# Products wider than 128 columns walk their moving operand and their bank in two interleaved halves

## The chip, the core and the metric

The kernel runs on one core of one Trainium2 chip. The metric is the device time of one execution in microseconds, as the median of several runs. The engines of the core work beside each other, each on its own queue: TensorE multiplies matrices (the profile calls the products PE and the loads of their stationary operand PEld), VectorE (DVE) and ScalarE (ACT) work elementwise, GpSimd (POOL) takes some elementwise work, SyncE (SP) issues most DMAs. A matmul holds its stationary operand (up to 128 x 128) in the array, streams the columns of its moving operand past it from SBUF, and adds or writes the result into one bank of PSUM, 512 fp32 columns wide. The profiler records one execution.

## What is computed

One decoder block on x (1024 tokens x 1024 channels, fp32). Two branches read one normalised input, are gated and projected together; then follow a cross-attention into 256 memory tokens, a SwiGLU feed-forward layer and a last norm. Cut to what matters:

```python
u = rms_norm(h, norm_mix)
proj = u @ w_in                                    # u_ssm, q, k, v, f_logit, gate_logits
y_ssm = gelu(s5_ssm(u_ssm, ...))                   # diagonal state-space scan in 32 groups
glu_a, glu_b = split(y_ssm @ w_glu)
out_a = glu_a * sigmoid(glu_b)
out_b = forgetting_attention(q, k, v, f_logit + b_forget) @ w_fox_o   # causal, 8 heads of 64
h = h + (gate_a * out_a + gate_b * out_b) @ w_mix_out
h = h + memory_cross_attention(rms_norm(h), rms_norm(mem), w_mem_q, w_mem_kv, w_mem_o)
f_a, f_b = split(rms_norm(h) @ w_ffn_in)           # 1024 -> 2 x 2816
h = h + (silu(f_a) * f_b) @ w_ffn_out
out = rms_norm(h, norm_final)
```

## The kernel before

Every fp32 operand of a large product is split into a high part, rounded to the type fp32r that TensorE takes in one pass, and a low part, the rest (`Block.split`, L186: a ScalarE cast and a VectorE subtraction). A product is then three fp32r matmuls into one bank: high x high, high x low, low x high (`Block.mm3`, L175, with its three matmuls on L177, L178 and L179). `gemm_t` (L181) calls `mm3` for each 128-row slice of the contraction.

The work runs in stages, one behind the other with some overlap: the norms and transposes with the first projections (`stage_in`, whose order is written out by hand in `ORDER_IN`; there the profile puts all operations on L126, the line of the helper that keeps the order), gates and state-space branch (`stage_ssm`), the forgetting attention (`Fox`), the gated merge, mixing projection and cross-attention (`stage_tail`), and the feed-forward layer at its end. The mixing projection and both feed-forward projections use seven block products instead of eight, so they have matmul lines of their own: `mix_mm` (L660), `prod` (L1014, 22 hidden blocks x 7 block products x 12 matmuls) and `o_mm` (L1161, 7 block products x 11 x 12 matmuls). In the attention, `row_max` (L1767) computes scores once for the row maximum, `scores` (L1794 and L1795) computes them again transposed, and `values_hi` and `values_lo` (L1819, L1820, L1826) multiply the exponentials by the values. There the stationary operand has 64 or 65 columns, and on the diagonal a product has 128, 256, 384 or 512 moving columns. `values_of_v` has products of 264 and 256 columns, `keys` and `mem_scores` of 256. All others of these lines have 512.

In all of them the moving operand is a contiguous row of fp32 elements in each SBUF partition, and so is the stretch of the bank that it is written to. Bank use rotates over the names `mm`, `sc`, `pv` and `misc` (L130). Transposes and the small fp32 products of the state-space branch (L1504, L1510, L1535, L1578, L1579), with 128 columns or fewer, call the engine directly, and so does `warm` (L253), a few bf16 products of 256 columns at the start that use no result.

Which matmul waits for which operand is put in by the framework, from the tiles that it reads and writes.

Of the kernel before, what the change touches and what calls it, by code (L numbers as in the profile page):

```python
# [19 lines left out]
P = 128  # L20
# [46 lines left out]
def f32(ap):  # L67
    return ap.bitcast(F32)
# [60 lines left out]
class Block:  # L129
    BANKS = {"mm": 3, "sc": 2, "pv": 2, "misc": 1}  # L130

    def __init__(self, ctx, tc):
        self.tc, self.nc = tc, tc.nc
        nc = self.nc
        self.V, self.A, self.G, self.T, self.S = nc.vector, nc.scalar, nc.gpsimd, nc.tensor, nc.sync
        self.const = ctx.enter_context(tc.tile_pool(name="const", bufs=1))
# [32 lines left out]
    def wblock(self, w, k0, nk, c0, nc_, pool_lo=False, behind=None):  # L169
# [2 lines left out]
        hi, lo = self.wload([(0, (nk, nc_), src)], nk * nc_, pool_lo, behind)  # L172
        return tuple(t[:, :nk * nc_].rearrange("p (k c) -> p k c", k=nk) for t in (hi, lo))

    def mm3(self, ps, lh, ll, rh, rl, first, last):  # L175
        T = self.T
        T.matmul(ps, lh, rh, start=first, stop=False)  # L177
        T.matmul(ps, lh, rl, start=False, stop=False)  # L178
        T.matmul(ps, ll, rh, start=False, stop=last)  # L179

    def gemm_t(self, ps, wh, wl, act, h, nk, k0=0):  # L181
        for k in range(nk):
# [49 lines left out]
    def turn(self, xs, b, bank):  # L232

        ps = self.bank(bank)
        for k in range(4):
            self.T.transpose(ps[:, k * P:(k + 1) * P], xs[:, (4 * b + k) * P:(4 * b + k + 1) * P], self.ident)
        return ps
# [15 lines left out]
    def warm(self, n):  # L253
# [3 lines left out]
        for _ in range(n):  # L257
            self.T.matmul(ps[:, :2 * P], one[:, :P], one, start=True, stop=True)

# [313 lines left out]
def stage_tail(B, big, s2, sh, x, glu, aT, gate_d, kv_d, sums_d, w_fox_o, w_mix_out, g_mq, w_mem_q, w_mem_o, g_ffn,  # L573
               w_ffn_in, w_ffn_out, g_fin, out):
    nc, V, A, G, T, S, small, ident = B.nc, B.V, B.A, B.G, B.T, B.S, B.small, B.ident
# [5 lines left out]
    def slot(dt=F32, name="t"):  # L581
        return s2.tile([P, D], dt, tag="t", bufs=NS2, name=name)
# [69 lines left out]
    def mix_mm(n, i):  # L652
        ps = msets[n in (2, 7, 4)][i]
        for kk in range(2):
            wh, wl = mixw[n][kk]
            hi, lo = [a[kk][:, :, i * P:(i + 1) * P]
                      for a in part[(None, "A11", "A12", "S4", "A22", "S1", "S2", "S3")[n]]]
            for k in range(2):
                for m, (l_, r_) in enumerate(((hi, wh), (hi, wl), (lo, wh))):
                    T.matmul(ps, l_[:, k, :], r_[:, k, :], start=n in (1, 2, 7) and kk == k == m == 0,  # L660
                             stop=kk == k == 1 and m == 2, skip_group_check=True)

    def mix_add(n, i):
# [77 lines left out]
    for i in range(2):  # L741
        mix_mm(1, i)
    minuend(7)
    fox_part(6)
    mix_mm(1, 2)
    mix_weights(2)
    fox_part(7)
    mix_mm(1, 3)
    msets.append([B.bank(t_) for t_ in ("sc", "sc", "pv", "pv")])

# [56 lines left out]
    kth, ktl, vh, vl = [slot(F32R, "kv") for _ in range(4)]  # L807
# [200 lines left out]
    def prod(j, n, ps, first):  # L1008
        wh, wl = [t_.rearrange("p (k c) -> p k c", k=4) for t_ in wts.pop((j, n))]
        hi, lo = comb[(None, "A11", "A12", "S4", "A22", "S1", "S2", "S3")[n]]  # L1010
        for k in range(4):
            rh, rl = hi[k // 2][:, k % 2, :], lo[k // 2][:, k % 2, :]
            for i, (l_, r_) in enumerate(((wh, rh), (wh, rl), (wl, rh))):
                T.matmul(ps, l_[:, k, :], r_, start=first and k == 0 and i == 0, stop=k == 3 and i == 2,  # L1014
                         skip_group_check=True)

    def start(j):
        b1, b2 = ev[j, "b1"], _ = B.bank("mm"), B.bank("sc")
        prod(j, 1, b1, True)
        a0 = ev[j, "a0"] = sh.half("a0")  # L1020
        A.copy(a0, b1)
        prod(j, 2, b2, True)
        V.tensor_add(a0, a0, b2)
        A.activation(a0, a0, AF.Silu)

    def middle(j):
        b1 = ev[j, "b1"]
        b3 = ev[j, "b3"] = B.bank("pv")
        prod(j, 6, b1, False)
        a1 = ev[j, "a1"] = sh.half("a1")  # L1030
        A.copy(a1, b1)
        prod(j, 7, b3, True)
        prod(j, 5, b1, False)
        c1 = ev[j, "c1"] = sh.half("c1")
        ev["last"] = A.copy(c1, b1)
        V.scalar_tensor_tensor(out=c1, in0=c1, scalar=-1.0, in1=b3, op0=ALU.mult, op1=ALU.subtract)
# [118 lines left out]
    def o_mm(m, i):  # L1155
        n, p = seq[m]
        hi, lo = ops[m]
        ps = sets[n in (2, 7, 4)][i]
        gi = slice(i * P, (i + 1) * P)
        for k, (l_, r_) in enumerate(((hi, hi), (hi, lo), (lo, hi))):  # L1160
            T.matmul(ps, l_[:, gi], r_[:, 512:], start=n < 3 and p == 0 and k == 0 or n == 7 and p == 0 and k == 0,  # L1161
                     stop=p == NP - 1 and k == 2, skip_group_check=True)

    def o_add(n, i):
# [55 lines left out]
    for i in range(4):  # L1220
# [4 lines left out]
        r = refine() if i else None  # L1225
# [9 lines left out]
class Glu:  # L1235
# [11 lines left out]
    def product(self, j, h, b):  # L1247
        ps = self.B.bank("mm" if b == 0 else None)
        self.B.gemm_t(ps, *self.w[j], self.yT, h, 4, k0=4 * b)
        if j not in self.out:  # L1250
            self.out[j] = self.sh.tmp("sg")

        return ps.rearrange("p (t c) -> p t c", t=4), \
            self.out[j].rearrange("p (c t) -> p t c", t=8)[:, 4 * h:4 * h + 4, :]
# [338 lines left out]
class Fox:  # L1593
# [158 lines left out]
    def row_max(self, h):  # L1752

        B = self.B
        K1, K2, Q1, Q2 = self.hb[h % 2]

        def unit(qb, b):  # L1760
            if qb == 0:
                self.mc[h] = B.small.tile([P, 2, NT], F32, name="mc")
                B.V.memset(self.mc[h][:, 1, :], -3.0e38)
            mc = self.mc[h]
            n = min(512, (qb + 1) * P - 512 * b)
            ps = B.bank("mm")
            B.T.matmul(ps[:, :n], Q1[0:68, qb * P:(qb + 1) * P], K1[0:68, 512 * b:512 * b + n], start=True, stop=True)  # L1767
            if b == qb // 4:
                B.V.tensor_tensor_reduce(out=B.junk[:, :n], in0=ps[:, :n], in1=self.tri[:, 512 - n:512], scale=1.0,
                                         scalar=-3.0e38, op0=ALU.add, op1=ALU.max, accum_out=mc[:, 0, qb:qb + 1])  # L1770
            else:
                B.V.tensor_reduce(out=mc[:, 1, qb:qb + 1], in_=ps, axis=AX.X, op=ALU.max)

        return [lambda qb=qb, b=b: unit(qb, b) for qb in range(NT) for b in range(qb // 4 + 1)]
# [11 lines left out]
    def scores(self, h, qc, kt):  # L1786
        B, fp = self.B, self.fp
        V, A, G, T = B.V, B.A, B.G, B.T
        K1, K2, Q1, Q2 = self.hb[h % 2]
        off = max(0, kt * P - 512 * qc)  # L1790
        q = slice(512 * qc + off, 512 * qc + 512)
        k = slice(kt * P, (kt + 1) * P)
        ps = B.bank("sc")
        T.matmul(ps[:, off:], K1[0:69, k], Q1[0:69, q], start=True, stop=False)  # L1794
        T.matmul(ps[:, off:], K2[:, k], Q2[:, q], start=False, stop=True)  # L1795
        if kt * P >= 512 * qc:
            V.tensor_add(ps[:, off:off + P], ps[:, off:off + P], self.trk)  # L1797
        ph = self.sh.half("ph", F32R)
        pl = fp.tile([P, 512], F32R, tag="pl", bufs=4, name="pl")
        pf = self.sh.half("pf")  # L1800
        self.exp = A.activation(pf[:, off:], ps[:, off:], AF.Exp)  # L1801
        if (qc, kt) in ((0, 2), (1, 0), (1, 2), (1, 4)):
            self.mark = V.tensor_copy(ph[:, off:], pf[:, off:])  # L1803
            G.tensor_sub(pl[:, off:], pf[:, off:], f32(ph[:, off:]))  # L1804
        else:
            A.copy(ph[:, off:], pf[:, off:])  # L1806
            V.tensor_sub(pl[:, off:], pf[:, off:], f32(ph[:, off:]))  # L1807
        self.hi_todo.append((h, qc, kt, off, ph, pl))

    def values_hi(self):  # L1810
        u = h, qc, kt, off, ph, pl = self.hi_todo.pop(0)
        self.lo_todo.append(u)
        if kt == 0:
            if qc == 0:
                self.num[h] = self.fp.tile([65, L], F32, tag="num", name="num")
            self.pvs[h, qc] = self.B.bank("pv")
        ps = self.pvs[h, qc]
        va, vl = self.vh[kt // 2][:, kt % 2, h, :], self.vl[kt // 2][:, kt % 2, h * DH:(h + 1) * DH]
        self.B.T.matmul(ps[0:65, off:], va, ph[:, off:], start=kt == 0, stop=False)  # L1819
        self.B.T.matmul(ps[0:64, off:], vl, ph[:, off:], start=False, stop=False)  # L1820

    def values_lo(self):
        h, qc, kt, off, ph, pl = self.lo_todo.pop(0)
        ps = self.pvs[h, qc]
        last = kt == 4 * qc + 3
        self.B.T.matmul(ps[0:65, off:], self.vh[kt // 2][:, kt % 2, h, :], pl[:, off:], start=False, stop=last)  # L1826
        if last:
            self.B.A.copy(self.num[h][:, 512 * qc:512 * qc + 512], ps[0:65, :])
            if qc == 1:
                self.finish(h)  # L1830
# [158 lines left out]
```

## Time and profile before

| | us |
|---|---|
| median of three runs | 1555.63 (1554.66 to 1558.96) |
| span of the profiled execution, first to last instruction | 1552.1 |
| TensorE products busy in it | 1516.8 |
| TensorE loads of stationary operands busy | 1247.0 |
| VectorE busy | 1056.2 |
| ScalarE busy | 672.7 |
| GpSimd busy | 244.2 |

The profiled execution's span is 3.5 us under the median of the runs; what lies around the first and the last instruction is in the runs' time and not in the span. Busy time of TensorE is the time in which at least one matmul is under way. Matmuls overlap: one begins while the one before it is still draining, and their ends are modelled, so the mean duration that a group of matmuls shows is longer than the step from one start to the next. The step from start to start is what counts for time; it is read from the order of time (starts in the timeline, or the length of a run of matmuls in the chain of work that ended last divided by their number). The trace names the shape of each matmul as stationary rows * columns, then the moving operand's partitions x columns.

### The profile page before, as it was taken

What the parts mean: (1) busy time and instruction counts of PE and PEld (TensorE: products, weight loads), DVE (VectorE), ACT (ScalarE), POOL (GpSimd) and SP (SyncE); (2) the same over time, 40 slices, a digit from 0 to 9 for tenths busy, and PEclk for the clock granted to TensorE, in tenths of its full rate; (3) what the DMA queues carried; (4) which work ended last, traced back from release to release, by engine and by line L of the source; (5) the groups of instructions that cost most, each with busy time, mean ns of one, the idle gap of its engine ahead of it and who ended that gap; (6) DMA issues with size and microseconds to landing.
All of it is one profiled execution on the core that took longest, in us unless ns stands there. A gap on an engine that the chain in (4) does not pass through costs nothing.

```text
span 1552.1 us, 20558 instructions
## 1 busy us (share of the span) xinstructions
PE 1516.8 (98%) x7271; PEld 1247.0 (80%) x7271; DVE 1056.2 (68%) x1895; ACT 672.7 (43%) x1202; POOL 244.2 (16%) x323
## 2 busy tenths in 40 slices
PE   8999999999999899999999999999999999999997
PEld 7787888898777668888888778888888888888886
DVE  7666855554788686788756787777777776566555
ACT  6424333423666653444445654333333333354343
POOL 1045432200212123210102100000000000101001
PEclk9999999999999999999999999999999999999999
DMA  9465657642113647778421375454555554896642
GB/s 296 119 136 110 190 158 152 189 131 29 35 36 65 163 111 244 248 236 320 136 95 55 136 265 207 160 161 158 163 160 160 161 163 145 297 385 218 192 161 109
DMA packets 203177, 258.19 MB, mean 166 GB/s; under 512 B 36457, under 2 KB 127497, under 8 KB 202562
## 3 DMA queue, kind: packets, MB, share of 16 engines
q1 hardware_dynamic: 195874, 240.10, 51.7%
q10 hardware_dynamic: 7200, 16.78, 2.8%
q8 instruction: 57, 0.93, 0.2%
q14 instruction: 46, 0.38, 0.1%
HBM read 175.56 MB, written 83.20 MB: 167 GB/s over the span
## 4 chain that ended last, share of the span: by engine, by line
PE 78%; DVE 8%; DMA 5%; issue 3%; POOL 3%; ACT 2%; SPq 1%; POOLq 0%; ACTq 0%; DVEq 0%
PE mm L1014 15%; PE pv L1014 8%; PE mm L177 6%; PE mm L178 5%; PE mm L179 5%; PE mm L1161 5%; PE sc L1161 4%; PE mm L126 4%; PE sc L1014 3%; PE pv L1161 3%; PE sc L178 2%; PE sc L177 2%; PE sc L179 2%; PE misc L1161 2%; PE pv L178 1%
## 5 line engine op out<-in xcount | busy, mean ns | idle before, releaser
L188 DVE TENSOR_TENSOR wlo<-raw,whi 128x1024 fp32r<-128x1024 f32 (+2 forms) x119 | 127.1, 1070 | 90.9 <-ACT whi L187 90.6
L187 ACT CAST whi<-raw 128x1024 fp32r<-128x1024 f32 (+2 forms) x119 | 107.1, 904 | 116.8 <-DMA raw<-in_w_ffn_in_dram 25.4
L188 DVE TENSOR_TENSOR ol<-or,oh 128x1024 fp32r<-128x1024 f32 x73 | 91.9, 1266 | 67.1 <-ACT oh L187 66.0
L187 ACT CAST oh<-or 128x1024 fp32r<-128x1024 f32 x73 | 76.7, 1053 | 99.2 <-PE mm L1161 33.3
L177 PE MATMUL mm<-uh,whi 128*128 128x512 f32 x280 | 111.7, 399 | 0.5 <-ACT whi L187 0.5
L179 PE MATMUL mm<-uh,wlo 128*128 128x512 f32 x280 | 109.9, 393 | 0.5 <-DVE wlo L188 0.5
L178 PE MATMUL mm<-ul,whi 128*128 128x512 f32 x280 | 110.3, 394 | 0.0
L1046 POOL TENSOR_TENSOR g<-a,c 128x512 f32<-128x512 f32 x22 | 36.2, 1644 | 381.7 <-ACT a L1045 362.6
L1804 POOL TENSOR_TENSOR pl<-pf,ph 128x512 fp32r<-128x512 f32 (+1 forms) x32 | 39.7, 1240 | 241.6 <-DVE ph L1803 195.4
L206 POOL TENSOR_TENSOR r<-ms,mhalf 128x1 f32<-128x1 f32 (+1 forms) x30 | 20.5, 686 | 330.3 <-DVE ms L202 261.0
L1801 ACT ACTIVATE pf<-sc 128x512 f32<-128x512 f32 (+1 forms) x96 | 46.5, 490 | 45.8 <-DVE sc L1797 26.7
L179 PEld LDWEIGHTS mm<-uh,wlo 128*128 128x128 f32 x280 | 52.9, 189 | 12.3 <-DVE wlo L188 1.5
L177 PEld LDWEIGHTS mm<-uh,whi 128*128 128x128 f32 x280 | 53.0, 189 | 10.5 <-ACT whi L187 0.9
L178 PEld LDWEIGHTS mm<-ul,whi 128*128 128x128 f32 x280 | 53.1, 189 | 8.7
L1014 PE MATMUL pv<-S3h,we 128*128 128x512 f32 x176 | 58.2, 390 | 0.1
L1274 POOL TENSOR_TENSOR sg<-sg,ga 128x512 f32<-128x512 f32 x16 | 31.2, 1971 | 69.8 <-DMA ga<-gate_d 40.9
L1807 DVE TENSOR_TENSOR pl<-pf,ph 128x512 fp32r<-128x512 f32 (+2 forms) x64 | 35.0, 548 | 10.1 <-ACT ph L1806 9.3
L1161 PE MATMUL mm<-oh 128*128 128x512 f32 x106 | 41.2, 389 | 0.0
L1161 PE MATMUL mm<-oh,ol 128*128 128x512 f32 x106 | 41.2, 389 | 0.0
L1161 PE MATMUL mm<-ol,oh 128*128 128x512 f32 x106 | 41.2, 389 | 0.0
L177 PE MATMUL mm<-yh,whi 128*128 128x512 f32 x104 | 40.8, 393 | 0.0
L177 PE MATMUL sc<-uh,whi 128*128 128x512 f32 x104 | 40.8, 392 | 0.0
(714 smaller groups left out, 4673.4 us busy)
## 6 DMA issues: line engine op xcount, KB each, us to landing
or<-c_d SPq DMA_DIRECT2D x77, 256.0 KB
wo<-in_w_ffn_out_dram SPq DMA_DIRECT2D x22, 512.0 KB
c_d<-g SPq DMA_DIRECT2D x44, 256.0 KB
t_d<-wo SPq DMA_DIRECT2D x44, 256.0 KB
or<-t_d SPq DMA_DIRECT2D x44, 256.0 KB
raw<-in_w_ffn_in_dram SPq DMA_DIRECT2D x20, 512.0 KB
rawb<-in_w_ffn_in_dram SPq DMA_DIRECT2D x20, 512.0 KB
raw<-in_w_in_dram SPq DMA_DIRECT2D x18, 512.0 KB
```

The costliest lines, as they stand in the source:

```text
L126: return lambda *a, **k: self.tc.keep_in_program_order(op(*a, **k))
L177: T.matmul(ps, lh, rh, start=first, stop=False)
L178: T.matmul(ps, lh, rl, start=False, stop=False)
L179: T.matmul(ps, ll, rh, start=False, stop=last)
L187: self.copied = self.A.copy(hi, src)
L188: self.lowered = (self.G if pool_lo else self.V).tensor_sub(lo, src, f32(hi))
L1014: T.matmul(ps, l_[:, k, :], r_, start=first and k == 0 and i == 0, stop=k == 3 and i == 2, skip_group_check=True)
L1046: G.tensor_mul(g[:, 512:], a1, c1)
L1161: T.matmul(ps, l_[:, gi], r_[:, 512:], start=n < 3 and p == 0 and k == 0 or n == 7 and p == 0 and k == 0, stop=p == NP - 1 and k == 2, ski ...
L1801: self.exp = A.activation(pf[:, off:], ps[:, off:], AF.Exp)
L1804: G.tensor_sub(pl[:, off:], pf[:, off:], f32(ph[:, off:]))
L1807: V.tensor_sub(pl[:, off:], pf[:, off:], f32(ph[:, off:]))
```

## The change

A new method `product` takes the place of the direct call of the engine's `matmul`. Where the result has over 128 columns, it hands the engine the same bank and the same moving operand with another order of columns: the n columns are seen as two halves of n/4 pairs each, and the walk goes pair by pair, one pair of the first half, then one of the second half. For n = 512 the order of columns is 0, 1, 256, 257, 2, 3, 258, 259 and so on. Both sides have the same order, so that each result lands where it did. Number and order of the instructions, the stationary operands, the tiles and everything on the other engines stay.

```diff
+    def product(self, ps, l, r, start, stop, **kw):
+
+        n = ps.shape[-1]
+        if n > P and len(r.shape) == 2:
+            ps, r = (ap.rearrange("p (b a c) -> p a b c", b=2, c=2) for ap in (ps, r))
+        self.T.matmul(ps, l, r, start=start, stop=stop, **kw)
+
     def mm3(self, ps, lh, ll, rh, rl, first, last):
-        T = self.T
-        T.matmul(ps, lh, rh, start=first, stop=False)
-        T.matmul(ps, lh, rl, start=False, stop=False)
-        T.matmul(ps, ll, rh, start=False, stop=last)
+        self.product(ps, lh, rh, first, False)
+        self.product(ps, lh, rl, False, False)
+        self.product(ps, ll, rh, False, last)
...
-                    T.matmul(ps, l_[:, k, :], r_[:, k, :], start=n in (1, 2, 7) and kk == k == m == 0,
+                    B.product(ps, l_[:, k, :], r_[:, k, :], start=n in (1, 2, 7) and kk == k == m == 0,
...
-                T.matmul(ps, l_[:, k, :], r_, start=first and k == 0 and i == 0, stop=k == 3 and i == 2,
+                B.product(ps, l_[:, k, :], r_, start=first and k == 0 and i == 0, stop=k == 3 and i == 2,
...
-            T.matmul(ps, l_[:, gi], r_[:, 512:], start=n < 3 and p == 0 and k == 0 or n == 7 and p == 0 and k == 0,
+            B.product(ps, l_[:, gi], r_[:, 512:], start=n < 3 and p == 0 and k == 0 or n == 7 and p == 0 and k == 0,
...
-        T.matmul(ps[:, off:], K1[0:69, k], Q1[0:69, q], start=True, stop=False)
-        T.matmul(ps[:, off:], K2[:, k], Q2[:, q], start=False, stop=True)
+        self.B.product(ps[:, off:], K1[0:69, k], Q1[0:69, q], start=True, stop=False)
+        self.B.product(ps[:, off:], K2[:, k], Q2[:, q], start=False, stop=True)
```

The calls on L1767, L1819, L1820 and L1826 are replaced in the same way.

More of the change, by code (lines that the diff above doesn't have):

```diff
@@ L1766, in unit @@
             ps = B.bank("mm")
-            B.T.matmul(ps[:, :n], Q1[0:68, qb * P:(qb + 1) * P], K1[0:68, 512 * b:512 * b + n], start=True, stop=True)
+            B.product(ps[:, :n], Q1[0:68, qb * P:(qb + 1) * P], K1[0:68, 512 * b:512 * b + n], start=True, stop=True)
             if b == qb // 4:
@@ L1818, in values_hi @@
         va, vl = self.vh[kt // 2][:, kt % 2, h, :], self.vl[kt // 2][:, kt % 2, h * DH:(h + 1) * DH]
-        self.B.T.matmul(ps[0:65, off:], va, ph[:, off:], start=kt == 0, stop=False)
-        self.B.T.matmul(ps[0:64, off:], vl, ph[:, off:], start=False, stop=False)
+        self.B.product(ps[0:65, off:], va, ph[:, off:], start=kt == 0, stop=False)
+        self.B.product(ps[0:64, off:], vl, ph[:, off:], start=False, stop=False)
     def values_lo(self):
@@ L1825, in values_lo @@
         last = kt == 4 * qc + 3
-        self.B.T.matmul(ps[0:65, off:], self.vh[kt // 2][:, kt % 2, h, :], pl[:, off:], start=False, stop=last)
+        self.B.product(ps[0:65, off:], self.vh[kt // 2][:, kt % 2, h, :], pl[:, off:], start=False, stop=last)
         if last:
```

## The prediction

> **What bounds the kernel.** I read the page first (busy shares, chain), then busy time by stretches, then the chain in order of time.
>
> ```profile
> span 1552.1 us, 20558 instructions
> ...
> PE 1516.8 (98%) x7271; PEld 1247.0 (80%) x7271; DVE 1056.2 (68%) x1895; ACT 672.7 (43%) x1202; POOL 244.2 (16%) x323
> ...
> PE 78%; DVE 8%; DMA 5%; issue 3%; POOL 3%; ACT 2%; SPq 1%; POOLq 0%; ACTq 0%; DVEq 0%
> ```
>
> TensorE products are under way in 1516.8 of 1552.1 us and hold 78% of the chain. All other engines together can give back 35 us at most. By stretches (columns: us, then busy us and number for PE, PEld, DVE, ACT, POOL, then granted clock, DMA share, GB/s):
>
> ```profile
> 0.00:380.00 380.00, 365.83 (x1990) 311.71 (x1991) 230.19 (x498) 142.98 (x244) 96.14 (x209) 1.00 0.61 154
> 380.00:600.00 220.00, 212.00 (x1020) 160.15 (x1020) 164.53 (x387) 130.56 (x248) 40.40 (x33) 0.99 0.36 90
> 600.00:912.00 312.00, 308.56 (x1481) 254.67 (x1479) 234.28 (x416) 148.50 (x332) 57.50 (x47) 1.00 0.55 184
> 912.00:1330.00 418.00, 416.51 (x1842) 343.70 (x1842) 298.49 (x440) 158.78 (x269) 34.43 (x22) 1.00 0.53 175
> 1330.00:1552.00 222.00, 213.89 (x944) 176.74 (x942) 128.74 (x157) 91.83 (x112) 15.72 (x13) 0.99 0.64 223
> ```
>
> In no stretch is another engine busy above 76%, and the clock is granted in full. So the step from one product to the next sets the time. It is read from the chain in order of time (start, length, what):
>
> ```profile
> 1002.51 5.44 PE mm L1014 x24
> ...
> 1535.73 4.09 PE sc L1161 x18
> ```
>
> 24 products of 512 columns take 5.44 us, 18 take 4.09: **0.2267 us a product** in both. Traffic does not move it: the same number of products goes through 100 us with the DMA share at 0.85 as at 0.48.
>
> ```profile
> 1100.00:1200.00 100.00, 100.00 (x442) 82.78 (x442) 71.64 (x101) 35.34 (x56) 7.93 (x5) 1.00 0.48 154
> ...
> 1300.00:1400.00 100.00, 100.00 (x442) 82.66 (x441) 61.88 (x67) 41.72 (x52) 11.96 (x7) 1.00 0.85 303
> ```
>
> **What a column could cost.** The timeline has a few bf16 products of 256 columns that read half the bytes per column, one alone and a group of six:
>
> ```profile
> 11.23 0.27 PE L126 MATMUL mm<-ident 128*128 128x256 bf16 x1
> ...
> 11.23 0.82 PE L126 MATMUL mm<-ident 128*128 128x256 bf16 x6
> ```
>
> Five steps take 0.82 - 0.27 = 0.55 us, 0.110 each. Two of those are 0.220 us for 512 columns, 7 ns under the fp32r product. The attention has fp32r products with narrow stationary operands:
>
> ```profile
> 482.21 0.28 PE L1819 MATMUL pv<-ph,vhi 128*65 128x256 f32 x1
> 482.32 0.28 PE L1820 MATMUL pv<-ph,vlo 128*64 128x256 f32 x1
> 482.44 0.34 PE L1826 MATMUL pv<-pl,vhi 128*65 128x384 f32 x1
> ...
> 483.31 0.22 PE L1819 MATMUL pv<-ph,vhi 128*65 128x128 f32 x1
> 483.37 0.23 PE L1820 MATMUL pv<-ph,vlo 128*64 128x128 f32 x1
> 483.44 0.28 PE L1826 MATMUL pv<-pl,vhi 128*65 128x256 f32 x1
> 483.55 0.39 PE L177 MATMUL mm<-uh,whi 128*128 128x512 f32 x1
> ```
>
> From start to start: 128 columns 0.065 us (two steps in 0.13), 256 columns 0.115 (0.23 for two), 512 columns 0.2267. From 256 to 512 that is 0.1117 us, 0.436 ns a column, with 2 x 0.115 - 0.2267 = 3 ns left over for the handover. Taking the same 3 ns once from the two bf16 steps gives 0.220 - 0.003 = 0.217 us for 512 columns. So a 512-column product has a **surplus of some 10 ns** that grows with its columns, whatever the width of its stationary operand. It thus sits in the walk along the row, which is what the change alters. Two-digit times leave it uncertain by about 3 ns.
>
> The Trainium skill ("TensorE: Matmul & The Clock Gate", section "Back-to-back issue gap") has a warm product at columns / 2.4 + 2.5 ns, 215.8 ns for 512. The row says 226.7 for fp32r, so the trace disagrees for this type; by the page's figure the surplus would be 10.9 ns.
>
> **The change part by part.** It removes and adds no instruction, wait or transfer; it moves the order of columns within products of over 128. The stationary loads stay, and none of the moved products has another queue.
>
> How many: `prod`, `o_mm` and one of the lines of `mm3`, each over the whole span (count in brackets):
>
> ```profile
> 0.00:1552.00 1552.00, 421.06 (x1848) 346.32 (x1848) 1.00 0.55 166
> ...
> 0.00:1552.00 1552.00, 209.77 (x924) 173.43 (x924) 1.00 0.55 166
> ...
> 0.00:1552.00 1552.00, 330.30 (x880) 165.71 (x880) 1.00 0.55 166
> ```
>
> Products of 512 columns: 1848 + 924, `mix_mm` 7 x 4 x 12 = 336, L177 to L179 3 x 880 less 192 of 264 and 288 of 256 columns = 2160, `stage_in` 240, attention 6 lines x 48 = 288. Sum 5796. Besides, 96 of 384 and 672 of 256 or 264.
>
> No row shows a moving operand or a bank walked in pieces, so the price of the new order is bounded. Downward: the whole surplus goes, 10.7 ns (226.7 - 216; I put the floor of 0.217 at 0.216 since both bf16 steps are rounded). Upward: the nearest rows are ScalarE copies of 512 elements, all contiguous, written to SBUF eight elements apart, and read from PSUM eight apart:
>
> ```profile
> L1021 ACT COPY a<-mm 128x512 f32<-128x512 f32 x22 | 12.9, 585 | 20.6 <-PE mm L1014 20.6
> ...
> L1261 ACT COPY sg<-mm 128x512 f32<-128x512 f32 x8 | 9.0, 1156 | 0.0
> ...
> L126 ACT COPY us<-mm 128x512 f32<-128x512 f32 x8 | 4.7, 596 | 10.7 <-PE mm L126 10.7
> ```
>
> Single elements cost 1156 / 585 = 1.98 times on the SBUF side and 1.02 times on the PSUM side. Pairs make half as many jumps: an estimate of 1.49 times at worst, 338 ns a product. The ends are thus -10.7 and +111 ns. I take **-10.7**, because the surplus is proportional to the walk, independent of traffic and absent with half the bytes per column: it looks like consecutive columns that meet in one unit of memory, and two alternating regions 1 KB apart relieve that. This is a choice, not a measurement.
>
> Sum: 5796 x 10.7 ns = 62.0 us. The 96 of 384 columns give 5 ns each, 0.5 us. The 672 narrow ones with 128 stationary columns step in 0.120, 5 ns above the 0.115 of the narrow stationary operand, so something else than the walk is late there; 3 ns each, 2.0 us:
>
> ```profile
> 345.39 0.12 PE mm L177
> 345.51 0.12 PE mm L178
> ```
>
> Off the path: in 380 to 600 us the attention's exponentials and row maxima release TensorE (8 us without a product), and I count half of its gain of some 8 us, -4. Up to 100 us first loads and norms are awaited: -3. In the feed-forward layer nothing comes late: VectorE would go from 298.49/418 = 71% to 298.49/399 = 75%, DMA from 0.53 to 0.56. The stationary loads still fit:
>
> ```profile
> L1014 PEld LDWEIGHTS pv<-S3h,we 128*128 128x128 f32 x176 | 33.0, 188 | 7.4 <-ACT S3h L187 0.5
> ```
>
> 188 ns lies below 216 as it did below 227; where this cover fails, the gain stops at the load. Total 62.0 + 0.5 + 2.0 - 4 - 3 = 57.5: span 1552.1 - 57.5 = 1494.6, and with the 3.5 us by which the runs' median exceeds the span, **1498 us**.
>
> **Rivals.** *A, nothing measurable.* The surplus is a rate, so many bytes per ns from SBUF, or a per-column price of fp32r itself, and order does not enter; or the pattern is turned back into a plain one before it reaches the chip. For it: the step is constant to three digits over hundreds of us, as a rate would be. Against: nothing that the trace shows. 1555.6 us.
>
> *B, slower: each jump between the halves is paid.* The place is the fetch of the moving operand: two neighbouring pairs were one stretch of memory, now they lie 1 KB apart, and 512 columns make 255 jumps. It decides from a price of 10.7 / 255 = 0.04 ns a jump. If the surplus is paid for entering a stretch, and each stretch is now entered twice as often, it doubles: 5796 x 10.7 = +62 us, 1618 (B1). If pairs cost what half of ScalarE's excess says, 5796 x 111 ns = +643 us, 2199 (B2). For it: L1261. Against: L126 reads a bank in steps at 1.02.
>
> The Trainium skill speaks for B in "PSUM — Partial Sum Buffer" (Specifications): 8-byte lines, and any non-contiguous pattern slows matmuls significantly. "Advanced Engine Details and Errata" (PSUM Cachelines) asks only that every two consecutive elements be contiguous, and its section SBUF Cachelines for two hits on a 16-byte line; pairs meet both, which would be A. No row of this trace decides between the sentences.
>
> **How the numbers follow.** Forecast 0.45; A 0.26; B 0.29, of which B1 and prices near it 0.14 and B2 and beyond 0.15. About 0.3% (5 us) is what a measurement can tell from no change here. Faster 0.45, same 0.26, slower 0.29. The forecast's own range is 1484 (all 5796 at 11.2 ns, the others at 8, nothing lost: 65 + 6 = 71 us) to 1545 (one sixth of the gain). Cases of both signs are open, so the range for 8 in 10 reaches through A and B1: 1484 to 1640; B2 stays out.
>
> **What would show it.** Chain: 24 products of L1014 in 5.2 us (forecast), 5.44 (A), 5.7 (B1), 8.1 (B2). The 128-column steps of 0.065 must not move. TensorE's busy time should fall by about what the span falls, and in 380 to 600 us by less per product. Wrong would be: a step of 512 columns that does not change, a surplus that stays while 256-column products gain, or loads of stationary operands that end after the product before them.

## The result, and the profile after

The changed kernel takes 2172.14 us (median of 4 runs, 2169.94 to 2172.32) where the kernel before takes 1557.26 (4 runs beside them, 1554.66 to 1558.96): a ratio of 1.395, with a 95% interval of 1.392 to 1.397. The forecast was 1498 us with a range of 1484 to 1640; the time lies outside of it, on the slow side. Medians in this document are of all runs; ratios leave out one run, of `e6_sixtyfours`, which took 6047.91 us.

The page of the changed kernel, in the same lines as the page before (busy time and number of instructions by engine, then the chain that ended last):

```profile
span 2168.1 us, 20567 instructions
...
PE 2153.8 (99%) x7271; PEld 1327.8 (61%) x7271; DVE 1067.2 (49%) x1895; ACT 675.9 (31%) x1202; POOL 232.4 (11%) x323
...
PE 98%; DVE 1%; issue 1%; ACT 0%; POOL 0%; DMA 0%; POOLq 0%; DVEq 0%; ACTq 0%
```

The same 7271 products and loads, and the other engines do the same work in the same time (VectorE 1067.2 us against 1056.2, ScalarE 675.9 against 672.7). All of the new time is in TensorE's products, which now hold 98% of the chain instead of 78%. The chain in order of time shows the step (start, length, what; `product` has put all of these calls on L180):

```profile
1415.94 4.00 PE pv L180 x12
1419.94 8.00 PE mm L180 x24
```

24 products of 512 columns take 8.00 us where they took 5.44: **0.3333 us a product** against 0.2267, 106.7 ns more, or 0.417 ns for each of the 256 pairs. Nothing else is late, as the next stretches show: 301 products go through 100 us whether VectorE is busy for 51 of them or for 36 (columns as in the stretches shown of before).

```profile
1300.00:1400.00 100.00, 100.00 (x301) 58.50 (x300) 51.40 (x72) 25.75 (x41) 6.36 (x4) 1.00 0.37 118
...
2000.00:2100.00 100.00, 100.00 (x301) 58.50 (x300) 35.53 (x33) 28.95 (x34) 0.00 (x0) 1.00 0.40 131
```

Products that the change leaves alone hardly moved. The timeline of the attention has 128 columns at 0.065 us (two steps from 561.68 to 561.81), as before, while 256 columns went from 0.115 to about 0.165 (558.12 to 558.45). Over all products of 128 columns with 64 or 65 stationary ones, the median step behind another of 128 columns is 60 ns in both traces, and behind a wider product it went from 59 to 67 ns:

```profile
558.12 0.34 PE L180 MATMUL pv<-ph,vhi 128*65 128x256 f32 x1
558.29 0.34 PE L180 MATMUL pv<-ph,vlo 128*64 128x256 f32 x1
558.45 0.42 PE L180 MATMUL pv<-pl,vhi 128*65 128x384 f32 x1
...
561.68 0.23 PE L180 MATMUL pv<-ph,vhi 128*65 128x128 f32 x1
561.75 0.23 PE L180 MATMUL pv<-ph,vlo 128*64 128x128 f32 x1
561.81 0.34 PE L180 MATMUL pv<-pl,vhi 128*65 128x256 f32 x1
```

The steps from start to start, added up by width in both traces, account for the whole difference of the spans: products of 512 columns 1353.2 to 1941.1 us (+587.8), of 256 columns 63.3 to 82.5 (+19.2), of 264 columns 23.2 to 32.6 (+9.4), of 384 columns 21.1 to 24.9 (+3.9), the rest -4.3; together +616.0, and 2168.1 - 1552.1 = 616.0.

### The profile page after: what moved, and what is told of

Read it like the earlier page. It is cut to its first block, busy times and chain, and to the rows that moved or that the text cites. A ratio compares the mean times of both kernels' runs of the same rounds, so it can differ in the third digit from the quotient of the medians.

```text
span 2168.1 us, 20567 instructions
## 1 busy us (share of the span) xinstructions
PE 2153.8 (99%) x7271; PEld 1327.8 (61%) x7271; DVE 1067.2 (49%) x1895; ACT 675.9 (31%) x1202; POOL 232.4 (11%) x323
## 4 chain that ended last, share of the span: by engine, by line
PE 98%; DVE 1%; issue 1%; ACT 0%; POOL 0%; DMA 0%; POOLq 0%; DVEq 0%; ACTq 0%
PE mm L180 48%; PE sc L180 21%; PE pv L180 19%; PE mm L126 4%; PE misc L180 3%; PE sc L126 1%; PE misc L845 0%; PE pv L1585 0%; PE pv L1541 0%; PE pv L1584 0%; PE misc L1516 0%; PE misc L242 0%; PE pv L126 0%; PE misc L126 0%; PE pv L242 0%
## 5 line engine op out<-in xcount | busy, mean ns | idle before, releaser
L180 PE MATMUL mm<-uh,whi 128*128 128x512 f32 x280 | 143.0, 511 | 0.0
L180 PE MATMUL mm<-ul,whi 128*128 128x512 f32 x280 | 142.1, 507 | 0.0
L180 PE MATMUL mm<-uh,wlo 128*128 128x512 f32 x280 | 141.7, 507 | 0.0
L1052 POOL TENSOR_TENSOR g<-a,c 128x512 f32<-128x512 f32 x22 | 35.3, 1604 | 574.4 <-ACT a L1051 574.4
L180 PE MATMUL pv<-S3h,we 128*128 128x512 f32 x176 | 77.6, 502 | 0.0
L180 PEld LDWEIGHTS mm<-uh,wlo 128*128 128x128 f32 x280 | 55.0, 196 | 36.9 <-issue 1.1
L180 PEld LDWEIGHTS mm<-uh,whi 128*128 128x128 f32 x280 | 54.9, 196 | 32.6 <-DVE mc L1775 0.4
L180 PEld LDWEIGHTS mm<-ul,whi 128*128 128x128 f32 x280 | 54.9, 196 | 31.3 <-issue 0.5
L180 PE MATMUL mm<-oh 128*128 128x512 f32 x106 | 53.2, 502 | 0.0
L180 PE MATMUL mm<-ol,oh 128*128 128x512 f32 x106 | 53.2, 502 | 0.0
L180 PE MATMUL mm<-oh,ol 128*128 128x512 f32 x106 | 53.2, 502 | 0.0
L180 PE MATMUL sc<-uh,whi 128*128 128x512 f32 x104 | 53.2, 512 | 0.0
L180 PE MATMUL sc<-ul,whi 128*128 128x512 f32 x104 | 53.1, 510 | 0.0
L180 PE MATMUL sc<-uh,wlo 128*128 128x512 f32 x104 | 53.1, 510 | 0.0
L180 PE MATMUL mm<-yh,whi 128*128 128x512 f32 x104 | 52.3, 503 | 0.0
```

The source lines that it names most:

```text
L180: self.T.matmul(ps, l, r, start=start, stop=stop, **kw)
L1052: G.tensor_mul(g[:, 512:], a1, c1)
```

## The experiments

The theory after the result was that each change of place within the walk costs TensorE time. Three questions were open: on which side it is paid (the read of the moving operand from SBUF or the write to the bank), what is counted (jumps, or pieces of memory fetched), and whether another order could win the 10 ns that the plain walk has above 0.216 us.

The two feed-forward projections have seven block products each, with 132 products of the out projection in a row and 12 of the in projection at a time. So one kernel can give each block product an order of its own, and its step is read from the trace. In the rows below, a stretch of the out projection counts the products under way in it, one or two more than its length divided by the step; the mean step behind it is that of 120 products from start to start. Steps within the in projection are the length of 12 products in the chain, divided by 12. In these runs all other products walk plainly; `e3_fours` and `e6_sixtyfours` instead change one number of the changed kernel. Each was run once, but for `e6_sixtyfours` with ten runs.

### Which side pays (e1_sides)

```diff
-        n = ps.shape[-1]
-        if n > P and len(r.shape) == 2:
-            ps, r = (ap.rearrange("p (b a c) -> p a b c", b=2, c=2) for ap in (ps, r))
+        r, ps = [self.walk(ap, o) for ap, o in zip((r, ps), order)]
...
+ORDER_FFN_IN = {1: ('', ''), 2: ('h4', ''), 6: ('', 'h4'), 7: ('h8', ''), 5: ('', 'h8'), 3: ('h32', 'h32'), 4: ('h64', 'h64')}
+ORDER_FFN_OUT = {1: ('', ''), 2: ('h2', ''), 6: ('', 'h2'), 7: ('h2', 'h2'), 5: ('h4', 'h4'), 4: ('h8', 'h8'), 3: ('h16', 'h16')}
```

For each block product stands the order of the read, then that of the write: empty is the plain walk, `h4` takes groups of four columns from the two halves in turn, as the change does with two.

> All products walk plainly, as before the change, except those of the two feed-forward lines, where each of the seven block products has an order of its own; one-sided orders put the result's columns in other places, which changes values and not times. Feed-forward out: block product 1 plain, 2 pairs on the read side (SBUF) only, 6 pairs on the write side (PSUM) only, 7 pairs on both, 5 fours on both, 4 eights on both, 3 sixteens on both. Feed-forward in: 1 plain, 2 fours read only, 6 fours written only, 7 eights read only, 5 eights written only, 3 thirty-twos on both, 4 sixty-fours on both. The changed kernel's 512-column step of 0.3333 us against 0.2267 is 256 jumps at 0.417 ns, one TensorE cycle each. Theory R (the read pays per jump): pairs read only 0.333, written only 0.227, fours read only 0.280, written only 0.227, eights read only 0.253. Theory W (the bank pays per jump): the same with read and written exchanged. Theory M (a jump costs on the slower of both sides, either alone is enough): 0.333 for all three kinds of pairs. Theory P (it is the pattern of three dimensions, not the jumps): every order but the plain one 0.333. By jumps on both sides: fours 0.280, eights 0.253, sixteens 0.240, thirty-twos 0.233, sixty-fours 0.230.

The out projection by stretches, in the order of its block products 1, 2, 6, 7, 5, 4, 3:

```profile
1350.00:1375.00 25.00, 25.00 (x112) 20.68 (x111) 13.03 (x14) 5.90 (x6) 2.14 (x1) 1.00 0.85 312
1385.00:1415.00 30.00, 30.00 (x90) 17.45 (x89) 12.72 (x11) 10.09 (x10) 0.00 (x0) 1.00 0.87 315
1425.00:1450.00 25.00, 25.00 (x112) 20.71 (x111) 15.91 (x12) 10.95 (x12) 4.21 (x2) 1.00 0.71 227
1460.00:1490.00 30.00, 30.00 (x90) 17.47 (x89) 8.59 (x7) 7.40 (x7) 0.00 (x0) 1.00 0.41 125
1500.00:1530.00 30.00, 30.00 (x122) 22.68 (x121) 12.60 (x12) 11.17 (x11) 0.00 (x0) 1.00 0.54 170
1535.00:1560.00 25.00, 25.00 (x104) 19.51 (x103) 11.03 (x9) 8.83 (x9) 0.00 (x0) 1.00 0.46 147
1565.00:1590.00 25.00, 25.00 (x106) 19.80 (x105) 11.99 (x27) 5.22 (x11) 2.06 (x3) 1.00 0.23 85
```

Compare the first with the third row: 112 products in 25 us whether the bank is written plainly or by pairs, a mean step of 226.7 ns in both. Compare the second with the fourth: 90 in 30 us, 340.0 ns, whether the bank joins in or not. **The read pays all of it and the write nothing**: theory R has the side right, W and M fall. The in projection says the same of larger groups (block products 5 and 1 together, then 2, 3, 4, 6, 7):

```profile
1006.19 5.45 PE mm L180 x24
1011.64 3.01 PE sc L180 x12
1014.65 2.84 PE mm L180 x12
1017.49 2.72 PE pv L180 x12
1020.21 2.72 PE mm L180 x12
1022.93 2.92 PE pv L180 x12
```

Fours written take 2.72 us for 12, eights written and the plain ones 5.45 for 24, as ever; fours read take 3.01, eights read 2.92, thirty-twos 2.84 and sixty-fours 2.72. The pattern of three dimensions as such (theory P) falls with the sixty-fours. But the price is not proportional to the jumps either, as theory R had it (0.280 for fours, 0.253 for eights): pairs cost 106.7 to 113 ns for 256 jumps, fours 23 ns for 128 (250.0), eights 17 for 64 (243.3), sixteens 13 for 32 (240.0). Something sets pairs apart from all the rest.

### Steps in place of halves, and rereading (e2_steps)

```diff
+        if kind == "s":
+            return ap.rearrange("p (a b c) -> p b a c", b=n // 2, c=2)
+        if kind == "k":
+            return ap[:, :n].unsqueeze(1).to_broadcast([P, 512 // n, n])
...
+ORDER_FFN_IN = {1: ('', ''), 2: ('s4', 's4'), 6: ('s8', 's8'), 7: ('s16', 's16'), 5: ('s4', ''), 3: ('', 's4'), 4: ('s16', '')}
+ORDER_FFN_OUT = {1: ('', ''), 2: ('k2', ''), 6: ('k4', ''), 7: ('k16', ''), 5: ('k64', ''), 4: ('', 's16'), 3: ('s64', 's64')}
```

`s4` walks pairs at a step of four columns, in two passes; `k2` reads the first two columns again and again.

> As the run before, with other orders on the feed-forward lines; those that reread a few columns leave the rest of the operand out of the product. Feed-forward in: block product 1 plain, 2 pairs at a step of four columns in two passes on both sides, 6 at a step of eight in four passes, 7 at a step of sixteen in eight passes, 5 step four read only, 3 step four written only, 4 step sixteen read only. Feed-forward out: 1 plain, 2 reads the same two columns 256 times, 6 the same four 128 times, 7 the same sixteen 32 times, 5 the same sixty-four 8 times (the bank is written plainly), 4 step sixteen written only, 3 pairs of halves 64 wide at a step of sixty-four on both. If a jump costs the same whatever its distance, every order of pairs has 0.333 on the side that pays. If only far jumps pay, those at a step of four columns stay at 0.227. If the read pays for each new 16 bytes beyond what a plain walk fetches, steps of four already pay in full. Rereading: if what is left over the clock in the plain walk (0.2267 against 0.2133) is paid for entering new memory on the read side, the same two or four columns give 0.216; if it is paid on the write side or per product, 0.227; if going back is a jump like any other, two columns give 0.333, four 0.280, sixteen 0.240, sixty-four 0.230.

The in projection (block products 2, 3, 4, 6, 7, then 5 and 1 together):

```profile
1075.44 5.43 PE sc L180 x12
1080.87 2.74 PE mm L180 x12
1083.61 5.18 PE pv L180 x12
1088.79 5.54 PE mm L180 x12
1094.33 5.18 PE pv L180 x12
1099.51 8.15 PE mm L180 x24
```

Pairs at a step of four columns take 5.43 us for 12, 452 ns each: worse than the far jumps between halves, and **twice the plain walk**. Written at that step, the bank again costs nothing (2.74). A step of eight has 461 ns, of sixteen 431, and it does not matter whether the bank joins (block products 4 and 7 have 5.18 both). So near jumps are not cheaper; what is lost looks like the other half of what a fetch brings. The third of the three expectations, that steps of four already pay in full, had the direction, and none had the size. The dearest order of all is `s64`, pairs at a step of sixty-four columns on both sides, with a mean step of 486.7 ns, more than twice the plain walk; no run has its write side alone.

```profile
1810.00:1870.00 60.00, 60.00 (x124) 25.58 (x123) 15.44 (x37) 7.33 (x13) 3.33 (x6) 1.00 0.12 44
```

Of the rereading block products, those that read the same two or four columns step in 216.5 ns, 117 in 25 us; here are the plain one, the two and the four columns:

```profile
1630.00:1655.00 25.00, 25.00 (x112) 20.68 (x111) 12.61 (x14) 6.33 (x7) 2.14 (x1) 1.00 0.90 320
1660.00:1685.00 25.00, 25.00 (x117) 21.88 (x116) 16.34 (x14) 12.44 (x12) 0.00 (x0) 1.00 1.05 391
1690.00:1715.00 25.00, 25.00 (x117) 21.85 (x117) 16.55 (x13) 11.50 (x13) 4.45 (x3) 1.00 0.75 248
```

When only two or four columns are reread, the 10 ns of surplus are gone. So they do belong to the read of the moving operand. That they are the price of walking through memory at all, and not of walking in a row, is the reading of all runs together: no order tried that reads 512 different columns came below the plain step.

### Fours throughout (e3_fours)

```diff
-            ps, r = (ap.rearrange("p (b a c) -> p a b c", b=2, c=2) for ap in (ps, r))
+            ps, r = (ap.rearrange("p (b a c) -> p a b c", b=2, c=4) for ap in (ps, r))
```

> The changed kernel with groups of four columns in place of pairs on both sides, in all products of over 128 columns: 128 jumps in 512 columns. If jumps are what costs, half of the excess: 5796 x 53 ns = 309 us over before, span about 1860. If it is lines of 16 bytes fetched twice that cost, fours fetch each once: span about 1552. If it is the three-dimensional pattern: as the changed kernel, 2168.

One run took 1676.07 us, beside 1561.34 of the kernel before. The step is 250.0 ns in both projections: 12 products in 3.00 us.

```profile
1117.11 3.00 PE sc L180 x12
1120.11 3.00 PE mm L180 x12
```

Neither of the simple predictions met it: half of the jumps would have left some 1860 us, fetches of 16 bytes alone 1552. Doubling the group took away four fifths of the excess, which suits the filling of 16 bytes as the larger part, and something smaller for the change of stream stays.

### What is fetched (e4_reads)

```diff
+        if kind == "q":
+            return ap.rearrange("p (b a c) -> p a b c", b=4, c=n)
+        if kind == "t":
+            return ap.rearrange("p (a b c) -> p b a c", b=2, c=n)
...
+            at = 512 - SHIFT.get(n, 0)
+            l_ = l_[:, :1].to_broadcast([P, P]) if n in CONST else l_[:, gi]
+            B.product(ps, l_, r_[:, at:at + 512], order=ORDER_FFN_OUT[n], ...)
```

`q2` takes pairs in turn from four quarters, `t4` every second group of four columns and then the others; `SHIFT` begins the row so many columns earlier, and `CONST` names the block products whose stationary is one column repeated.

> As the two runs before, all on the read side only; values change with it. Feed-forward in: block product 1 rereads the same eight columns, 2 the same thirty-two; 6, 7, 5, 3 and 4 read every second group of 4, 8, 16, 32 and 64 columns in a first pass and the others in a second. Feed-forward out: 1 plain with one stationary column repeated 128 times, 2 pairs of halves with the same, 6 pairs in turn from four quarters, 7 fours from four quarters, 5, 4 and 3 plain but from 2, 4 and 16 columns earlier in the tile. Theory F (the read fetches a unit of 16 bytes in 1.667 ns and keeps only the last): groups of 4 and more at a step fetch no unit twice and stay at 0.227; pairs from quarters cost 256 units, 0.44; fours from quarters 0.227. Theory J (each jump costs 0.417 ns as in the halves): groups of 4 at a step 0.28, of 8 0.253, of 16 0.240; pairs from quarters 0.333, fours 0.28. Theory U (the unit is larger, and a group that does not fill it wastes the rest): groups at a step cost up to twice 0.2133, some 0.44, until the group fills the unit, 0.227 from there on. The surplus of the plain walk: if it comes from the stationary load's reads, 0.216 with one repeated stationary column; if it hangs on where the row begins, it changes with the shift; else 0.227 in all four. Rereading eight columns 0.216, thirty-two 0.227 or above.

Two stretches of the out projection, pairs from quarters and fours from quarters:

```profile
1425.00:1475.00 50.00, 50.00 (x114) 23.39 (x113) 15.45 (x12) 10.17 (x12) 3.43 (x2) 1.00 0.37 122
1485.00:1515.00 30.00, 30.00 (x114) 21.85 (x113) 11.97 (x11) 9.96 (x10) 0.00 (x0) 1.00 0.52 172
```

114 products take 50 us in one and 30 us in the other: 443.3 ns against 268.0. Theory F had 440 and 227, theory J 333 and 280. So F has the pairs, and the fours, which J has nearly, cost 41 ns more than F allows. The walks in two passes decide against J (block products 4, 6 and 7 of the in projection, which read every second group of 64, 4 and 8 columns):

```profile
1020.14 2.76 PE pv L181 x12
1022.90 2.77 PE mm L181 x12
1025.67 2.80 PE pv L181 x12
```

Every second group of 4, 8, 16, 32 and 64 columns steps in 231, 233, 240, 237 and 230 ns, near the plain 227, where J had 280 for the fours. So the unit is not larger than four columns, and theory U falls as well. Pairs from the two halves with one repeated stationary column, block product 2, took 326.7 ns. The surplus of the plain walk hangs neither on the stationary load (231 with one repeated stationary column) nor on the row's beginning (230 to 233 from 2, 4 and 16 columns earlier). Eight columns reread had 215 and thirty-two 237.7.

### Distance, and groups of 64 (e5_apart, e6_sixtyfours)

`e5_apart` takes its two streams of 256 columns from places further apart in the tile; `e6_sixtyfours` is the changed kernel with `c=64` in products whose width is a multiple of 128.

> Read side only, values changed by it: two streams of 256 columns, taken in turn, that lie further apart than the halves' 256 columns. Feed-forward out, pairs: distance 256 (control), 260, 264, 272, 288, 384 and 512 columns for block products 1, 2, 6, 7, 5, 4, 3. Feed-forward in, distance 512: groups of 2, 4, 8, 16, 32, 64 columns for block products 1, 2, 6, 7, 5, 3; 4 plain. Theory F, the read fetches 16 bytes in four TensorE cycles (1.667 ns): pairs from halves had 0.333 to 0.340, which is 192 fetches for 128 units, so half of the second visits still find their unit. If what is kept depends on the place of the two units against each other, the step changes with the distance between 0.227 (all kept, 128 fetches) and 0.440 (none kept, 256). If it is a matter of the order of visits alone, all distances have 0.333 to 0.340. Of groups at distance 512: 0.25, 0.243, 0.24, 0.237, 0.227 for 4, 8, 16, 32, 64 as from halves if the distance does not enter. If alternation relieves a conflict at some distance, as the prediction had it, one of them lies below 0.2267.

By stretches of 35 us, pairs at the distances of 256, 264 and 512 columns:

```profile
1385.00:1420.00 35.00, 35.00 (x105) 20.34 (x104) 11.93 (x13) 10.61 (x10) 0.00 (x0) 1.00 1.01 363
...
1470.00:1505.00 35.00, 35.00 (x108) 20.87 (x108) 15.30 (x12) 10.34 (x12) 3.58 (x2) 1.00 0.54 166
...
1645.00:1680.00 35.00, 35.00 (x108) 20.93 (x107) 11.72 (x23) 4.59 (x8) 0.82 (x2) 1.00 0.14 51
```

Pairs at the distance of 256 columns stepped in 340.0 ns, and at 260, 264, 272, 288, 384 and 512 columns in 326.7, 326.7, 326.7, 328.3, 328.3 and 328.3. Groups of 4, 8, 16, 32 and 64 at distance 512 had 250.6, 243.5, 240.3, 236.6 and 230.3, much as from halves, and pairs in the in projection 333 (median). The distance decides some 13 ns of the 113 that the pairs cost here, and none of the places lies below the plain walk: no run shows a conflict between neighbours that another place relieves.

> The changed kernel with groups of 64 columns in place of pairs, in the products of 256, 384 and 512 columns (those of 264 stay plain); it computes what the reference does. If the price hangs on how often the read leaves a unit of 16 bytes before it is used up, nothing is left of the 616 us: 1552 to 1562 as before the change. If it hangs on a pattern of three dimensions or on far jumps by their number (8 in place of 256), 1555 + 616 x 8/256 = 1575.

The median of its ten runs is 1558.07 us against 1556.69 before (13 runs), a ratio of 1.0007 (95% interval 0.9993 to 1.0021), as the first of the two expectations had it. With whole stretches of 256 bytes, the interleave is free, on both sides; and it wins nothing.

### Whether the unit is 16 aligned bytes (e7_aligned)

The orders of the two passes again, on rows that begin 2 or 4 columns earlier in the tile (`SHIFT`).

> Feed-forward out only, read side only, values changed by it; all else plain. Every second group in a first pass and the others in a second. Block product 1: groups of 4 columns beginning on 16 bytes of the tile; 2: the same, the whole row 2 columns (8 bytes) earlier; 5: the same, 4 columns (16 bytes) earlier; 6: groups of 8, 2 columns earlier; 7: groups of 8, 4 columns earlier; 4: pairs at a step of four columns, two passes; 3: the same, 2 columns earlier. Theory F (units of 16 aligned bytes, 1.667 ns per fetch, the last one kept): a group of 4 that straddles two units costs two fetches: 1 and 5 0.231 as in the run before, 2 256 fetches, 0.427 plus the surplus of 10 to 20 ns, 0.44 to 0.45; 6 three units for 8 columns, 192 fetches, 0.33; 7 0.234 as without a shift; 4 and 3 0.45, since a pair lies in one unit either way. Theory G (the fetch takes any 16 bytes, aligned to 8): all groups of 4 0.231 and all of 8 0.234. Theory H (units of 32 bytes): 7 as 6, and 5 unlike 1.

By stretches, block products 1, 2, 6, 7, 5, 4, 3:

```profile
1336.00:1362.00 26.00, 26.00 (x114) 21.13 (x114) 13.01 (x15) 6.93 (x7) 2.14 (x1) 1.00 0.88 317
1367.00:1422.00 55.00, 55.00 (x123) 25.30 (x122) 16.26 (x15) 12.29 (x14) 0.00 (x0) 1.00 0.57 206
1427.00:1465.00 38.00, 38.00 (x118) 22.72 (x117) 15.03 (x13) 10.46 (x10) 1.83 (x1) 1.00 0.50 165
1470.00:1496.00 26.00, 26.00 (x113) 21.01 (x112) 11.21 (x10) 9.56 (x10) 0.00 (x0) 1.00 0.58 182
1501.00:1527.00 26.00, 26.00 (x114) 21.15 (x113) 11.36 (x10) 10.01 (x10) 0.00 (x0) 1.00 0.60 187
1532.00:1586.00 54.00, 54.00 (x121) 24.92 (x120) 12.36 (x11) 11.49 (x14) 0.00 (x0) 1.00 0.21 68
1591.00:1646.00 55.00, 55.00 (x122) 25.16 (x121) 14.96 (x36) 6.90 (x15) 2.91 (x5) 1.00 0.13 48
```

The first two rows hold the same number of columns in the same groups of four and differ by 8 bytes in where the row begins: 114 products in 26 us, 123 in 55, a step of 231.1 against 453.3 ns. Moved by 16 bytes (fifth row) the step is 231.1 again. Groups of eight that straddle three units have 326.7, aligned ones 233.3; pairs have 451.1 and 453.3 either way. All seven are theory F's, to within 4 ns of its 0.45 and 0.33, and G and H fall. **The read fetches 16 aligned bytes, four fp32 columns, at some 1.7 ns apiece** (an estimate: (453.3 - 231.1) / 128 units), which is also what 512 plain columns in 128 units come to (226.7 / 128 = 1.77).

## Why the prediction was wrong

- *What bounds the kernel*: right. The step between products set the time before and does so after; no wait, load or transfer came in between. Stationary loads stayed hidden (1327.8 us busy in 2168.1).
- *The surplus of some 10 ns, and its place in the walk along the row*: right in size and in place. 216.5 ns with two or four columns reread against 226.7 plain is 10.2 ns, on the read side; the prediction had 10.7 with an uncertainty of 3. Its way to that size was partly luck: it took 0.115 us for the narrow products of 256 columns from one pair of steps, but their median in that trace is 118 ns, and by the same sum the handover would have been 9 ns (2 x 118 - 226.7) and not 3, and the surplus some 16. Its bf16 product "alone" is the first of the group of six. The Trainium skill's 215.8 ns ("TensorE: Matmul & The Clock Gate", "Back-to-back issue gap") is reached by fp32r products of 512 columns only where two to eight columns are reread (216.5 and 215), not where the whole operand is read.
- *The step that failed* is the choice: "I take **-10.7**, because the surplus is proportional to the walk, independent of traffic and absent with half the bytes per column: it looks like consecutive columns that meet in one unit of memory, and two alternating regions 1 KB apart relieve that." Consecutive columns do meet in one unit, but that is what makes them cheap: four of them share one fetch. None of the three observations tells a conflict from a plain price of reading, and the choice took a conflict. Measured: +106.7 ns a product where the prediction had -10.7, for the larger part because a pair uses half of a 16-byte unit before the walk leaves it (e3, e7), and no distance (e5) and no group (e1, e4) below the plain step.
- *The upper end, +111 ns from the ScalarE rows*, was within 5 ns of what came. It was the nearest row, and the argument passed over it. Its two halves point the right way too: 1.98 times on the SBUF side and 1.02 on the PSUM side, as the read pays and the bank does not. That L1261 and the read have the same cause was not tested; L1261 writes. So the closeness of the number is luck as far as the runs show, and "at worst" does not hold: other orders of pairs cost 431 to 487 ns a product (e2, e4) against its 338.
- *Rival B* had the place (the fetch of the moving operand) and, as B2, the time: 2199 us against 2172.14. Its mechanism, a price for each jump, was not right: eight far jumps cost nothing (e6), near steps cost more than far jumps (452 against 333), and what counts is how many 16-byte fetches a row needs. Its chance of 0.15 and the end of the range at 1640 were the second fault. With ends that far apart and, in its own words, a choice and not a measurement between them, the range should have reached to the dearer one.
- *Rival A* falls: the order does enter. *B1* falls with it.
- *The sentences of the Trainium skill.* The Trainium skill ("PSUM — Partial Sum Buffer", Specifications) has any non-contiguous pattern slow a matmul; every order written alone here left the step at 226.7 to 230 ns, so the runs disagree for the write. The Trainium skill ("Advanced Engine Details and Errata", SBUF Cachelines) asks two hits of a 16-byte line in SBUF; the unit of 16 bytes agrees, but two hits are not enough for this type: pairs at a step of four columns have two and take 452 ns. The prediction set the section PSUM Cachelines of that page against the sentence on non-contiguous patterns; that section of the Trainium skill has the sentence too.
- *Widths and counts*: 5796 x 106.7 ns = 618 us; steps of 512 columns grew by 587.8. The other 30 us were waits before, which longer products now cover: beyond 226.7 ns apiece the steps of 512 columns added up to some 39 us before, and beyond 333.3 ns to some 8 us after. The time in which no product was under way fell from 35.3 us (1552.1 - 1516.8) to 14.3. The prediction let such waits eat 7 us of its gain; here they took 30 us off the loss. The 128-column steps moved by 8 ns or less in the median; the prediction had them stay.

Three things stay open. Alternating pairs need 256 fetches if nothing is kept and 128 if both units are; at 327 to 340 ns they cost what 192 fetches cost (326.7 in e7), so half of the second visits seem to find their unit, and no run shows why. Groups of four from halves or quarters pay 23 and 41 ns although each unit is fetched once; so 83 of the 106.7 ns go when a group fills its unit (e3), and the other 23, which wider groups bring down to nothing, have no cause shown. And pairs at a step of 4, 8, 16 and 64 columns should all need 256 fetches, but step in 452, 461, 431 and 487 ns.

## What to carry to other kernels

An fp32r operand that TensorE streams is best laid out so that each aligned 16 bytes are read in full, in one go, before the walk moves on (no other type was walked in pieces here). Half-used units made a product 1.4 to 2.1 times as long. Whole units cost 2 to 6% at a stride and 10 to 18% for fours taken in turn from two or four places. None of the orders in which the result alone was written to its bank cost more than 2%. A steady surplus is not yet a conflict: before rearranging a walk that all products share, time two or three orders in one stretch of the kernel. And where the nearest rows of a trace price an unknown access at half again as much, that price belongs in the range until something better is measured.

## What the runs showed of the hardware beyond that

Writing the bank alone in pairs at a step of four or sixteen columns, or in pairs, fours and eights from halves, leaves the step at 226.7 to 230 ns. Rereading is not free by itself: two or four columns 216.5 ns, eight 215 (median), but sixteen 241.9, thirty-two 237.7 and sixty-four 226.7, so going back over several units costs up to 15 ns more than going on. Eight columns are two units in turn, and change units as often as the plain walk does, yet they cost less (215 against 226.7); so a read seems to keep more than the last unit, unlike theory F. And the same order of pairs from halves stepped in 333.3 ns in the changed kernel, in 340.0 in e1 and e5, and in 326.7 in e4 with one repeated stationary column; why is not known.
